# Branch B's recurrence in a hybrid decoder block: per-chunk transition matrices in place of a chunk-by-chunk solve

## The chip, the cores and the metric

The kernel runs on one core of a Trainium2 chip. A core has TensorE (PE; its weight loads are listed as PEld), VectorE (DVE), ScalarE (ACT), GpSimd (POOL) and SyncE (SP), which here issues nearly all DMAs. Every engine works through its own instructions in a fixed order and waits on semaphores. The metric is device microseconds of one execution; lower is better.

## The reference

The block is one decoder layer over 16 learned tokens and 1024 tokens of width 1024: a half-step SwiGLU, then two mixers side by side (A, a gated DeltaNet with 8 heads of 128; B, RWKV-7 with 16 heads of 64), their gated sum through an output projection, a second half-step SwiGLU and a norm. The change concerns B's recurrence:

```python
def step(state, inp):
    r_t, w_t, k_t, v_t, a_t, b_t = inp
    sa = jnp.einsum('bhvk,bhk->bhv', state, a_t)
    state = state * w_t[:, :, None, :] + sa[..., None] * b_t[:, :, None, :] \
        + v_t[..., None] * k_t[:, :, None, :]
    return state, jnp.einsum('bhvk,bhk->bhv', state, r_t)
```

Per head the state is 64 x 64. Each token multiplies it by a decay, adds a rank-one term that depends on the state itself (`sa`) and one that does not, and reads an output out of it. Everything is float32.

## The kernel before, in words

The program has three stages: `ffn1`, `middle`, `ffn2`. Activations lie transposed, channels on partitions and tokens along the free axis. `middle` handles two segments of tokens (528 with the learned ones, then 512), and in each, one after another, eight channel blocks j of 128: one head of A and two heads of B, B's first head on partitions 0 to 63, its second on 64 to 127. Each pair of segment and j is a round `it`, sixteen in all.

A round's actions are written as functions, and `schedule()` (L162) gives their program order: `merge_blocks chains new_b+ new_a+ operands+ inverses+ gates finish`, where + marks the next round's. The order at the segment change (`SWITCH`) and in the last round (`FINAL`: `gates merge_blocks chains fill finish`, where `fill` is the output projection of the first segment) differ. That order is not the order of execution. A planner sorts each engine's instructions when the program is built: of what it takes to be ready by its own estimate, the one that is earliest in program order goes first. So `chains` of one round goes ahead of everything of the next, and where it waits by that estimate, projections (`pp`, 128x128 weights, 24 matmuls for one column tile and 512 tokens) and `operands` of the next round are put between its pieces. The order so found is fixed at run time.

**new_b, new_a** (L925, L1019) project and prepare B's and A's inputs. **operands** (L1060) makes, for all chunks of a round, the products that need no state: for B in chunks of CB = 64 tokens (NCB = 8 chunks), `LT` (from `grb`, L1076), `BKt` (transposes of `BK`, L1145), and in a loop over three kinds (L1154) `vka`, `yb` and `vbk`, the last multiplied by the chunk's decay `gam`. **inverses** (L1209) and **merge_blocks** (L1252) make the triangular inverses `Y` of all chunks, 64 x 64 for B, 128 x 128 for A, by way of DRAM (`scX`, `Xc`).

**chains** (L1292) runs through the chunks in order. `chunk_a` (four of them, 128 tokens each) and `chunk_b` (eight) are independent chains that alternate: B's chunk i, then A's chunk i/2 if i is even. `chunk_b` (L1347) takes the state `SB` (128 partitions x 64: two heads), and does, each for two heads by two 64x64 matmuls: `b1` = AR·SB; on DVE `rh` = b1 + vka; `b2` = Y·rh; on ACT `U`, its copy out of PSUM; `b3` = BKt·U; on DVE the new state, b3·gam + sg, where POOL has made sg = SB·gam + vbk meanwhile; and the outputs `bq` = SB·AR + U·LT, added to `yb` on DVE. Each product has a PSUM tile of the pool `ch`, which has two banks and also serves `merge_blocks`, `chunk_a` and `finish`. The pool `mx`, which `operands` uses, has two banks in the first segment and three in the second. A head's matmul with both operands on partitions 0 to 63 and its output there uses one quadrant of the PE array, the other head's the opposite one; the index pairs `HS` and `HX` choose the quadrants.

**gates, finish** (L1386, L1413) make the gates and the norms of both outputs and store the merged round; `finish` uses `yb`, and of the chain's tiles `BKt` as scratch.

Each fp32 matmul leaves two records in the trace.

## Time and profile before

| | us |
|---|---|
| median of 3 runs | 3180.59 |
| lowest, highest | 3179.36, 3185.57 |
| the profiled execution | 3186.03 |
| its span, first to last instruction | 3184.2 |
| one round of the second segment (1889.42 to 1979.64) | 90.22 |
| mean granted TensorE clock | 0.984 |

The profile page is one execution. Its second part shows the span in 40 slices, as tenths of busy time:

```profile
PE   5999999999999999999999999999999899999998
DVE  7554444346676676676767777777766755555335
ACT  4222222125555555454565455555544422222114
```

`middle` lies between slices 12 and 31: the first product of `chunk_b` starts at 914.9 us, the last one at 2399.5 us. A group of instructions (by line, engine, operation and tile) has its count after x, its busy time, the mean of one in ns, and the idle time of the engine before them. The chain that ended last is listed as pieces with a start, a length and a line. A row of windows gives a stretch, its length, and for PE, PEld, DVE, ACT and POOL the busy time with the number of instructions, then the granted clock, the share of DMA and GB/s.

### The profile page before, as it was taken

How to read it: one execution, taken by the hardware profiler on the slowest of the kernel's cores; microseconds unless marked ns; L12 is line 12 of the kernel's file. 1: busy time of each engine (PE TensorE's matmuls, PEld its weight loads, DVE VectorE, ACT ScalarE, POOL GpSimd, SP SyncE). 2: the span in 40 equal slices, each digit the busy share in tenths (PEclk: the TensorE clock that was granted, in tenths of full speed). 3: DMA queues.
4: the chain of work that ended last, by engine and by line, in shares of the span. 5: the costliest groups of instructions: out<-in, count | busy, mean ns of one | idle time of the engine just before them, and what ended most of it. 6: DMA issues, size and time to landing. Idle time of an engine off the chain costs nothing. (4 is left out here: it accounts for less than half of the span.)

```text
span 3184.2 us, 57962 instructions
## 1 busy us (share of the span) xinstructions
PE 3048.8 (96%) x23606; PEld 2523.7 (79%) x23606; DVE 1950.6 (61%) x3820; ACT 1321.8 (42%) x2260; POOL 551.2 (17%) x810
## 2 busy tenths in 40 slices
PE   5999999999999999999999999999999899999998
PEld 4999998998877877787776777777776688887886
DVE  7554444346676676676767777777766755555335
ACT  4222222125555555454565455555544422222114
POOL 4222220000011011110111111111101433222000
PEclk8999999999999999999999999999999999999999
DMA  2222224234222222222332232233344232224323
GB/s 93 95 93 81 81 84 160 77 94 143 60 68 72 74 72 59 72 71 75 96 92 71 70 82 71 71 79 78 96 149 165 67 99 86 80 82 150 104 79 111
DMA packets 256554, 286.93 MB, mean 90 GB/s; under 512 B 168272, under 2 KB 174416, under 8 KB 256288
## 3 DMA queue, kind: packets, MB, share of 16 engines
q1 hardware_dynamic: 252048, 271.42, 28.9%
q0 software_dynamic: 2512, 8.65, 0.7%
q8 instruction: 185, 3.03, 0.4%
q10 hardware_dynamic: 1728, 3.16, 0.3%
q14 instruction: 81, 0.66, 0.1%
HBM read 232.70 MB, written 50.47 MB: 89 GB/s over the span
## 5 line engine op out<-in xcount | busy, mean ns | idle before, releaser
L259 PE MATMUL pp<-uk,w 128*128 128x264 f32 (+1 forms) x4824 | 994.8, 354 | 7.6 <-DVE gg L1410 3.9
L259 PEld LDWEIGHTS pp<-uk,w 128*128 128x128 f32 x4824 | 747.8, 191 | 130.7 <-issue 22.1
L154 ACT ACTIVATE w<-wraw 128x1024 fp32r<-128x1024 f32 (+2 forms) x332 | 328.2, 989 | 709.8 <-PE pd L259 289.9
L259 PE MATMUL pd<-hd,w 128*128 128x512 f32 (+1 forms) x2640 | 499.6, 351 | 12.6 <-DVE w L155 5.7
L259 PEld LDWEIGHTS pd<-hd,w 128*128 128x128 f32 x2640 | 428.6, 189 | 82.4 <-DVE w L155 7.2
L422 PE MATMUL pg<-bt,w 128*128 128x260 f32 (+1 forms) x2772 | 456.8, 321 | 24.3 <-ACT bt L154 10.1
L422 PEld LDWEIGHTS pg<-bt,w 128*128 128x128 f32 x2772 | 400.3, 189 | 69.4 <-ACT bt L154 11.0
L428 DVE TENSOR_TENSOR c<-c,pg 128x520 f32<-128x520 f32 (+1 forms) x308 | 208.0, 689 | 361.3 <-PE pg L422 296.5
L155 DVE TENSOR_TENSOR w<-wraw,w 128x1024 fp32r<-128x1024 f32 (+2 forms) x332 | 382.6, 1153 | 67.6 <-ACT w L154 61.4
L422 PE MATMUL pg<-b,w 128*128 128x260 f32 (+1 forms) x2376 | 390.1, 320 | 10.1 <-POOL b L155 4.9
L422 PEld LDWEIGHTS pg<-b,w 128*128 128x128 f32 x2376 | 343.8, 189 | 45.1 <-POOL b L155 5.4
L392 POOL TENSOR_TENSOR wrx<-wrx 128x512 f32<-128x512 f32 x44 | 66.7, 1515 | 574.8 <-DVE w22b L155 306.5
L154 ACT ACTIVATE w<-wrx 128x1024 fp32r<-128x1024 f32 (+1 forms) x66 | 60.3, 913 | 182.6 <-PE pg L422 169.4
L1357 POOL TENSOR_SCALAR sgam<-SBn,gam 128x64 f32<-128x64 f32 x112 | 66.7, 595 | 393.1 <-DVE SBn L1371 371.7
L1230 DVE TENSOR_TENSOR Xb<-Xb,tb 115x126 f32<-115x126 f32 (+22 forms) x496 | 126.2, 254 | 11.9
L1228 DVE TENSOR_TENSOR tb<-Ub,Xb 115x126 f32<-115x126 f32 (+22 forms) x496 | 125.2, 252 | 11.0
L1039 DVE SCALAR_TENSOR_TENSOR acc<-xr,pk,acc 128x528 f32<-128x528 f32 (+1 forms) x144 | 108.8, 755 | 18.9 <-ACT acc L1035 17.5
L539 DVE SCALAR_TENSOR_TENSOR h<-pd,h 128x528 f32<-128x528 f32 (+1 forms) x64 | 44.6, 698 | 117.7 <-PE pd L259 117.7
L259 PE MATMUL pwo<-uk,w 128*128 128x512 f32 x384 | 106.2, 421 | 6.2 <-ACT rg L918 2.7
L539 DVE SCALAR_TENSOR_TENSOR hh<-pd,hh 128x512 f32<-128x512 f32 x64 | 44.2, 690 | 107.8 <-PE pd L259 106.7
L259 PEld LDWEIGHTS pwo<-uk,w 128*128 128x128 f32 x384 | 72.5, 196 | 26.0 <-ACT rg L918 3.5
L1371 DVE SCALAR_TENSOR_TENSOR SBn<-b,gam,sgam 128x64 f32<-128x64 f32 x128 | 36.2, 283 | 88.7 <-PE b L1354 87.6
(373 smaller groups left out, 4045.5 us busy)
## 6 DMA issues: line engine op xcount, KB each, us to landing
wraw<-in_win SPq DMA_DIRECT2D x150, 512.0 KB, 3.7
wraw<-in_wgu SPq DMA_DIRECT2D x44, 512.0 KB, 3.5
wrx<-in_wgu SPq DMA_DIRECT2D x44, 512.0 KB, 3.7
wraw<-in_wdn SPq DMA_DIRECT2D x48, 320.0 KB, 3.0
wraw<-in_wdn SPq DMA_DIRECT2D x32, 384.0 KB, 3.1
hid<-c SPq DMA_DIRECT2D x44, 260.0 KB, 4.0
hr<-hid SPq DMA_DIRECT2D x22, 520.0 KB, 9.9
hid<-c SPq DMA_DIRECT2D x44, 256.0 KB, 3.2
```

The lines of the kernel that those rows point to most:

```text
L154: g.nc.scalar.activation(hi, src, AF.Copy)
L155: (eng or g.nc.vector).tensor_tensor(lo, src, hi.bitcast(F32), op=ALU.subtract)
L259: g.nc.tensor.matmul(ps, lhsT=l, rhs=r, start=i == 0, stop=i == n - 1)
L392: nc.gpsimd.tensor_tensor(a22, a21, a22, op=ALU.add)
L422: nc.tensor.matmul(ps[:, c0 : c0 + cn], lhsT=l[:, x, k, :], rhs=r[:, k, y, c0 : c0 + cn], start=i == 0, stop=i == 3 * HK - 1)
L428: nc.vector.tensor_tensor(o, x, y, op=ALU.add)
L539: nc.vector.scalar_tensor_tensor(hv, pd, 0.5, hv, op0=ALU.mult, op1=ALU.add)
L1039: nc.vector.scalar_tensor_tensor(acc[:, :n], xr[:, tap : tap + n], V("convw", ct * 4 + tap), acc[:, :n], op0=ALU.mult, op1=ALU.add)
L1228: nc.vector.tensor_tensor(tv, U[:, i, i + 1 :].unsqueeze(2).to_broadcast([npt, nt, ncc]), X[:, i, 0:ncc].unsqueeze(1).to_broadcast([npt, n ...
L1230: nc.vector.tensor_tensor(X[:, i + 1 :, 0:ncc], X[:, i + 1 :, 0:ncc], tv, op=ALU.add)
L1357: nc.gpsimd.tensor_scalar(sg, SB, gam, None, op0=ALU.mult)
L1371: nc.vector.scalar_tensor_tensor(new, p3[:, :CB], gam, sg, op0=ALU.mult, op1=ALU.add)
```

## The change

For a chunk, the new state is an affine function of the old one. The change computes its matrix and its constant part for all eight chunks ahead, in a new function `transitions` that `chains` calls first, so that in series there is one product a chunk, and the outputs follow for all chunks at the end.

In `operands`, `at`, the transpose of AR's first half, is made by products with the identity, its matmuls alternating with those of `vka`; `yb` and `vbk` form the second alternating pair, and `vbk` leaves PSUM without the factor `gam`. In `transitions` there are six products over all chunks and both heads (32 records each): xa = Y·at and xv = Y·vka, copied out by ACT; mt = xa·BKt plus the unit matrix; vbk += BKt·xv, then times `gam` on POOL; AR's second half += xa·LT; yb += xv·LT (the four additions on DVE). A step is then: one product mt·SB of two 64x64 matmuls, and on DVE the new state product·gam + vbk. The states of all chunks are kept in `SBs`. After the loop, `bq` = SBs·AR over all chunks and one addition to `yb`. The tile `unit` is filled once, at the start of `middle`.

```diff
--- before.py
+++ after.py
@@ -722,6 +722,10 @@
         g.Ub = ms.tile([115, 32, 32], F32, name="Ub")
         for t in (*g.Y, g.XA, g.Ub):
             nc.gpsimd.memset(t, 0.0)
+
+        g.unit = ms.tile([P, CB], F32, name="unit")
+        for hp in HS:
+            nc.gpsimd.tensor_copy(g.unit[hp], g.C("ident")[hp, hp])
         g.bkpm = ms.tile([P, 2, 64], F32, name="bkpm")
         nc.gpsimd.memset(g.bkpm, 0.0)
         g.bkm = ms.tile([P, 64], F32, name="bkm")
@@ -1138,6 +1142,7 @@
     inverse_inputs(g, q)
 
     BKt = q.BKt = st.tile([P, NCB, 2, CB], F32, name="BKt", tag="BKt", bufs=2)
+    at = q.at = st.tile([P, NCB, CB], F32, name="at", tag="at")
     ps = [g.mx.tile([P, 512], F32, name="bkt", tag="mx") for _ in range(2)]
     for i in range(NCB):
         for y in range(2):
@@ -1148,19 +1153,29 @@
         nc.scalar.activation(BKt[:, :, y], ch3(ps[y], CB), AF.Copy)
 
     Vs = q.Vs
-    vka = q.vka = st.tile([P, NCB, CB], F32, name="vka", tag="vka")
-    vbk = q.vbk = st.tile([P, NCB, CB], F32, name="vbk", tag="vbk")
+    vka, vbk = (st.tile([P, NCB, CB], F32, name=x, tag=x) for x in ("vka", "vbk"))
+    q.vka, q.vbk = vka, vbk
     yb = q.yb = st.tile([P, FULL], F32, name="yb", tag="yb", bufs=2)
-    for kind in range(3):
-        ps = g.mx.tile([P, 512], F32, name="vp", tag="mx")
+
+    def kind(name, *ops):
+
+        ps = [g.mx.tile([P, 512], F32, name=name, tag="mx") for _ in ops]
         for i in range(NCB):
-            for hp, hx in HX:
-                l, r = ((LT[hx, i, 1, :CB], Vs[hx, i]), (Vs[hx, i], LT[hx, i, 1, CB:]), (BKt[hx, i, 1], Vs[hx, i]))[kind]
-                nc.tensor.matmul(ps[hp, i * CB : (i + 1) * CB], lhsT=l, rhs=r, start=True, stop=True)
-        if kind == 2:
-            nc.vector.tensor_tensor(vbk, ch3(ps, CB), q.gam.unsqueeze(2).to_broadcast([P, NCB, CB]), op=ALU.mult)
-        else:
-            nc.scalar.activation(yb if kind else vka.rearrange("p c m -> p (c m)"), ps, AF.Copy)
+            for p, op in zip(ps, ops):
+                for hp, hx in HX:
+                    l, r = op(i, hp, hx)
+                    nc.tensor.matmul(p[hp, i * CB : (i + 1) * CB], lhsT=l, rhs=r, start=True, stop=True)
+        return ps
+
+    ident = g.C("ident")
+    pa, pv = kind("vp", lambda i, hp, hx: (AR[hp, i, 0, :], ident[hp, hp]),
+                  lambda i, hp, hx: (LT[hx, i, 1, :CB], Vs[hx, i]))
+    nc.scalar.activation(at, ch3(pa, CB), AF.Copy)
+    nc.scalar.activation(vka, ch3(pv, CB), AF.Copy)
+    pr, pk = kind("vp", lambda i, hp, hx: (Vs[hx, i], LT[hx, i, 1, CB:]),
+                  lambda i, hp, hx: (BKt[hx, i, 1], Vs[hx, i]))
+    nc.scalar.activation(yb, pr, AF.Copy)
+    nc.scalar.activation(vbk, ch3(pk, CB), AF.Copy)
     if meta:
         btm = q.btm = st.tile([64, P], F32, name="btm", tag="btm")
         ps = g.mx.tile([P, 512], F32, name="btp", tag="mx")
@@ -1289,15 +1304,45 @@
     nc.vector.tensor_copy(Y[0:64, NCB:, 64:128], ch3(ps4[0:64, 0:256], 64))
 
 
+def transitions(g, q):
+
+    nc, st = g.nc, g.st
+    Y = g.Y[q.it % 2]
+    AR, LT, BKt, vbk, yb = q.AR, q.LT, q.BKt, q.vbk, q.yb
+    flat = lambda t: t.rearrange("p c m -> p (c m)")
+
+    def product(pool, name, op):
+        ps = getattr(g, pool).tile([P, 512], F32, name=name, tag=pool)
+        for i in range(NCB):
+            for hp in HS:
+                l, r = op(i, hp)
+                nc.tensor.matmul(ps[hp, i * CB : (i + 1) * CB], lhsT=l, rhs=r, start=True, stop=True)
+        return ps
+
+    xa, xv = (st.tile([P, NCB, CB], F32, name=x, tag=x) for x in ("xa", "xv"))
+    nc.scalar.activation(flat(xa), product("ch", "xp", lambda i, hp: (Y[hp, i, hp], q.at[hp, i])), AF.Copy)
+    nc.scalar.activation(flat(xv), product("ch", "xp", lambda i, hp: (Y[hp, i, hp], q.vka[hp, i])), AF.Copy)
+    mt = q.mt = st.tile([P, NCB, CB], F32, name="mt", tag="mt")
+    ps = product("ch", "mp", lambda i, hp: (xa[hp, i], BKt[hp, i, 0]))
+    nc.vector.tensor_tensor(mt, ch3(ps, CB), g.unit.unsqueeze(1).to_broadcast([P, NCB, CB]), op=ALU.add)
+    ps = product("ch", "np", lambda i, hp: (BKt[hp, i, 0], xv[hp, i]))
+    nc.vector.tensor_tensor(vbk, ch3(ps, CB), vbk, op=ALU.add)
+    nc.gpsimd.tensor_tensor(vbk, vbk, q.gam.unsqueeze(2).to_broadcast([P, NCB, CB]), op=ALU.mult)
+    ps = product("ch", "rp", lambda i, hp: (xa[hp, i], LT[hp, i, 0, CB:]))
+    nc.vector.tensor_tensor(AR[:, :, 1, :], ch3(ps, CB), AR[:, :, 1, :], op=ALU.add)
+    ps = product("ch", "yp", lambda i, hp: (xv[hp, i], LT[hp, i, 0, CB:]))
+    nc.vector.tensor_tensor(yb, ps, yb, op=ALU.add)
+
+
 def chains(g, q):
 
+    transitions(g, q)
     nc, st, c, j = g.nc, g.st, q.c, q.j
     meta = q.s == 0
     Y = g.Y[q.it % 2]
     S, SB = q.SA, q.SB
     Va, ktl, attn, egl = q.Va, q.ktl, q.attn, q.egl
     kqg = q.kq[:, :, q.off : q.off + FULL]
-    AR, LT, BKt = q.AR, q.LT, q.BKt
     hs = lambda h: slice(64 * h, 64 * h + 64)
     pt = lambda name: g.ch.tile([P, 512], F32, name=name, tag="ch")
     if meta:
@@ -1324,7 +1369,6 @@
         nc.tensor.matmul(ps[:, :P], lhsT=q.vkm[:, 1, :], rhs=vnm, start=True, stop=True)
         nc.vector.tensor_copy(S, ps[:, :P])
     oa = q.oa = kqg[:, 1, :]
-    yb, vka, vbk = q.yb, q.vka, q.vbk
 
     def chunk_a(i):
         csl = slice(i * CA, (i + 1) * CA)
@@ -1344,43 +1388,26 @@
         nc.vector.scalar_tensor_tensor(S, S, egl[:, i : i + 1], p3[:, :P], op0=ALU.mult, op1=ALU.add)
         nc.scalar.activation(oa[:, csl], pq[:, :CA], AF.Copy)
 
-    def chunk_b(i, SB):
-        gam, csl = q.gam[:, i : i + 1], slice(i * CB, (i + 1) * CB)
-
-        def mm(ps, *terms):
-
-            for k, (l, r) in enumerate(terms):
-                for hp in HS:
-                    nc.tensor.matmul(ps[hp, :CB], lhsT=l[hp], rhs=r[hp], start=k == 0, stop=k == len(terms) - 1)
-
-        sg = st.tile([P, CB], F32, name="sgam", tag="sgam", bufs=1)
-        nc.gpsimd.tensor_scalar(sg, SB, gam, None, op0=ALU.mult)
-        nc.gpsimd.tensor_tensor(sg, sg, vbk[:, i], op=ALU.add)
-        p1 = pt("b1")
-        mm(p1, (AR[:, i, 0, :], SB))
-        rh = st.tile([P, CB], F32, name="rhB", tag="rhB", bufs=1)
-        nc.vector.tensor_tensor(rh, p1[:, :CB], vka[:, i], op=ALU.add)
-        p2 = pt("b2")
+
+    SBs = st.tile([P, NCB + 1, CB], F32, name="SBs", tag="SBs")
+    nc.gpsimd.tensor_copy(SBs[:, 0], SB)
+    for i in range(NCB):
+        ps = pt("b1")
         for hp in HS:
-            nc.tensor.matmul(p2[hp, :CB], lhsT=Y[hp, i, hp], rhs=rh[hp], start=True, stop=True)
-        U = st.tile([P, CB], F32, name="Us", tag="Us", bufs=2)
-        nc.scalar.activation(U, p2[:, :CB], AF.Copy)
-        p3 = pt("b3")
-        mm(p3, (BKt[:, i, 0], U))
-        new = st.tile([P, CB], F32, name="SBn", tag="SBn", bufs=2)
-        nc.vector.scalar_tensor_tensor(new, p3[:, :CB], gam, sg, op0=ALU.mult, op1=ALU.add)
-        pq = pt("bq")
-        mm(pq, (SB, AR[:, i, 1, :]), (U, LT[:, i, 0, CB:]))
-        nc.vector.tensor_tensor(yb[:, csl], pq[:, :CB], yb[:, csl], op=ALU.add)
-        return new
-
-    for i in range(NCB):
-        SB = chunk_b(i, SB)
+            nc.tensor.matmul(ps[hp, :CB], lhsT=q.mt[hp, i], rhs=SBs[hp, i], start=True, stop=True)
+        nc.vector.scalar_tensor_tensor(SBs[:, i + 1], ps[:, :CB], q.gam[:, i : i + 1], q.vbk[:, i],
+                                       op0=ALU.mult, op1=ALU.add)
         if i % 2 == 0:
             chunk_a(i // 2)
+    ps = pt("bq")
+    for i in range(NCB):
+        for hp in HS:
+            nc.tensor.matmul(ps[hp, i * CB : (i + 1) * CB], lhsT=SBs[hp, i], rhs=q.AR[hp, i, 1, :],
+                             start=True, stop=True)
+    nc.vector.tensor_tensor(q.yb, ps, q.yb, op=ALU.add)
     if meta:
         nc.sync.dma_start(g.sdr[j][:, :P], S)
-        nc.sync.dma_start(g.sdr[j][:, P:], SB)
+        nc.sync.dma_start(g.sdr[j][:, P:], SBs[:, NCB])
 
 
 def gates(g, q):
```

## The prediction

> **What bounds the kernel now.** The page's first part and the windows come first: is one engine full in the stage that changes, or does the chain of state updates set the pace?
>
> ```profile
> PE 3048.8 (96%) x23606; PEld 2523.7 (79%) x23606; DVE 1950.6 (61%) x3820; ACT 1321.8 (42%) x2260; POOL 551.2 (17%) x810
> ```
> ```profile
> 1889.42:1979.64 90.22, 89.46 (x831) 66.33 (x832) 66.38 (x164) 49.19 (x92) 14.61 (x31) 1.00 0.31 79
> ```
> The second row is one whole round of the middle stage (one head index j of the second segment): 90.22 us, PE busy 89.46 of it, at granted clock 1.00; DVE 66.38, ACT 49.19. The round is PE's. While the chain of head j waits, PE runs the projections (`pp`) and operands of head j+1. So a shorter chain buys nothing by itself: what counts is PE time. The next view, the chain that ended last, shows what PE time a chunk costs (start, length, what).
>
> ```profile
> 1918.96 0.22 PE p L1332 x2
> 1919.18 0.94 PE pp L259 x4
> 1920.12 0.22 PE p L1336 x2
> 1920.34 0.22 PE pq L1340 x2
> 1920.56 0.47 PE pp L259 x2
> 1921.03 0.26 PE pq L1341 x2
> 1921.29 0.22 PE p L1343 x2
> 1921.51 0.70 PE pp L259 x3
> 1922.21 0.26 PE b L1354 x4
> 1922.47 0.66 PE pp L259 x2
> 1923.13 0.26 PE b L1365 x4
> 1923.39 0.67 PE pp L259 x2
> 1924.06 0.26 PE b L1354 x4
> 1924.32 0.23 PE bq L1354 x8
> 1924.55 0.43 PE pp L259
> ```
> ```profile
> 1950.19 1.92 PE vp L1159 x65
> ...
> 1952.69 12.16 PE pp L259 x52
> ```
> The reader is to see four prices. (1) A projection matmul in a run: 12.16 / 52 = 0.234 us. After one of A's groups it costs that as well (0.94 for 4). (2) After a group of B's it does not: 2 take 0.66 where 0.47 is due, 1 takes 0.43. So **each return from 64x64 matmuls to 128x128 ones costs 0.19 us**. (3) In a run, a record of B's 64x64 kind (one matmul leaves two records) costs 1.92 / 65 = 0.0295; a group of 4 right after projections takes 0.26 instead of 0.12: 0.14 to enter. One excursion of B costs 0.33 besides its work. (4) A chunk of A is 0.22 + 0.22 + 0.22 + 0.26 + 0.22 = 1.14 and pays no such price.
>
> A chunk of B makes three excursions (`b` L1354; `b` L1365; `b` and `bq` together): 3 x 0.26 + 0.23 + 3 x 0.19 = 1.58 us for 0.59 of work (20 records). The last round confirms it, where nothing but wout's `pwo` stands between the chunks:
>
> ```profile
> 2363.90:2399.90 36.00, 36.00 (x280) 24.21 (x278) 14.31 (x39) 9.02 (x21) 6.10 (x14) 1.00 0.47 160
> ```
> ```profile
> L259 PE MATMUL pwo<-uk,w 128*128 128x512 f32 x82 | 28.4, 437 | 0.0
> ```
> 36.0 - 82 x 0.234 (19.2) - 4 x 1.14 (4.6) = 12.2 us for eight chunks; 8 x 1.58 = 12.6, of which the first `b` (0.45) stands mostly ahead of the window. So among projections B costs 12.6 a round.
>
> **The change, part by part.** It removes, per round, `chunk_b`'s 80 matmuls (160 records, 4.7 us of work) in 24 excursions. It adds six products of 32 records, 8 steps of 4, one output run of 32, and 32 records for `at`: 288, or 128 more. PE has more work and fewer excursions.
>
> *Transitions.* If the six products stand in one run: 6 x 32 x 0.0295 = 5.66, and one excursion of 0.33: 6.0 us. *Steps:* 8 x (0.26 + 0.19) = 3.6; projections still stand between them, since each waits for the scalar_tensor_tensor of the one before. *Outputs:* 0.94 + 0.33 = 1.27. *`at`* is issued alternately with `vka`, and its rows and columns of the array are the two quadrants that `vka` leaves free. The nearest row with four quadrants in turn is `bkt`'s (start, length):
>
> ```profile
> 1556.91 0.98 PE L1145 MATMUL bkt<-ck,BK 64*64 64x64 f32 x52
> 1557.83 0.97 PE L259 MATMUL pp<-uk,w 128*128 128x512 f32 x3
> ```
> 0.92 / 52 = 0.0177 each, so the pair takes 64 x 0.0177 = 1.13 instead of 0.94: +0.19 (at most +0.94, if the quadrants don't overlap; I take 0.19, the same pattern). Sum added: **11.1 us**.
>
> *What is removed in an ordinary round.* Three chunks stand among projections (up to 1932.5), 3 x 1.58 = 4.7. The other five stand among the next head's `grb`, `bkt` and `vp`, 64x64 as well: such a chunk costs between its work (0.59) and 1.58, so 3.0 to 7.9. I take the middle, 5.4, as excursions are partly shared there but stalls come in. Removed: **10.2** (7.7 to 12.6). Against 11.1 that is +0.9.
>
> *A's chunks move.* With the chain done earlier, A's last two leave that stretch too, six groups whose excursions (0.33 each, up to 2.0) go; I take -1.0, half.
>
> *Evacuations and waits.* The prices:
>
> ```profile
> L1163 ACT ACTIVATE vka<-vp 128x512 f32<-128x512 f32 x16 | 9.6, 597 | 7.3 <-PE vp L1159 6.8 <-DVE rhB L1362 0.4
> L1161 DVE TENSOR_TENSOR vbk<-vp,gam 128x512 f32<-128x512 f32 x16 | 11.1, 691 | 38.9 <-PE vp L1159 36.7 <-POOL sgam L1358 1.5 <-POOL ELx L962 0.8
> L1109 POOL TENSOR_TENSOR E<-E,tk 128x512 f32<-128x512 f32 x16 | 16.8, 1051 | 13.8 <-ACT E L1103 9.9 <-ACT kts L1106 3.9
> L1367 ACT ACTIVATE Us<-b 128x64 f32<-128x64 f32 x128 | 28.6, 224 | 128.3 <-PE b L1365 128.0
> L1362 DVE TENSOR_TENSOR rhB<-b,vka 128x64 f32<-128x64 f32 x128 | 28.3, 221 | 21.2 <-PE b L1354 16.2
> L1374 DVE TENSOR_TENSOR yb<-bq,yb 128x64 f32<-128x64 f32 x128 | 27.5, 214 | 0.0
> L1358 POOL TENSOR_TENSOR sgam<-sgam,vbk 128x64 f32<-128x64 f32 x128 | 52.7, 412 | 22.4 <-DVE vbk L1161 12.5
> L1357 POOL TENSOR_SCALAR sgam<-SBn,gam 128x64 f32<-128x64 f32 x112 | 66.7, 595 | 393.1 <-DVE SBn L1371 371.7 <-DVE yb L1374 17.2 <-DVE tb L1228 4.2
> ```
> DVE: -8 x (0.221 + 0.214) - 0.69, +5 x 0.69 = -0.7 us a round. ACT: -8 x 0.224, +4 x 0.60 = +0.6. POOL: -8 x (0.60 + 0.41), +1.05 and a copy = about -7. None of the three is the bound, and no DMA is added or moved (the state's store keeps its place and size; `unit` is two copies, once). Only what they do to PE counts. Five of the six products wait for a bank or an operand that ACT (0.60) or DVE (0.69) must first evacuate, while PE runs the product before it (0.94): covered with 0.25 to spare, if the engine is free. It may be in one of the splits of weights:
>
> ```profile
> L154 ACT ACTIVATE w<-wraw 128x1024 fp32r<-128x1024 f32 (+2 forms) x332 | 328.2, 989 | 709.8 <-PE pd L259 289.9
> L155 DVE TENSOR_TENSOR w<-wraw,w 128x1024 fp32r<-128x1024 f32 (+2 forms) x332 | 382.6, 1153 | 67.6 <-ACT w L154 61.4
> ```
> Then 0.69 + 1.15 - 0.94 = 0.9 late: 0 to 4.5 us for five; I take 1.0, as DVE is in a split in about a tenth of a round (9 x 1.15 of 90) and otherwise in shorter work. The cover is the product itself; where it goes, a projection put in costs 0.33. In turn an `mt` or `vbk` add waiting at the head of DVE holds the split queued behind it, for which the projections wait; and `vbk`'s multiply on POOL holds the next head's `xr` copies by up to 1 us, which their convolution's slack takes up. Step 0's state needs that multiply (0.69 + 1.05 after its product); the two products behind (1.9) cover it. In the first segment `mx` has two banks, and each pair of `kind` needs both: up to two evacuations of 0.60 stand bare, twice; a projection put in makes that 0.33 each, inside the 1.0.
>
> **Sum:** +0.9 - 1.0 + 1.0 = +0.9 for 15 rounds, 13.5; in the last round 11.1 - 12.6 + 0.5 of stalls = -1.0. Together **+12 us**. The profiled execution took 3186.03 (its span is 3184.2): 3198. The median of the runs shown is 3180.59: **3192**.
>
> One wait could move as well:
>
> ```profile
> PE iv L1263 <- DMA Xc<-scX: 18.7, 7, 3.2
> ```
> In the first segment PE reaches `merge_blocks` before the inverses have come back from DRAM, 2.7 us in each of seven rounds. With no chain between the operands and that point PE may come earlier still, or the order may put more projections ahead: -18.7 to +18.7. I take 0; no row says which, and both ends are in the range.
>
> **The rivals.** *A, faster:* every excursion saved counts fully, the products run without a stall. Each of the 16 rounds gets the last one's 11.1 - 12.6 = -1.5: -24, so 3157. For it: that round's window; and PE's busy share covers some 8 us of entering and returning (24 x 0.33) in a round. Against it: five of eight chunks stand where excursions are shared. The Trainium skill's page Perfetto Trace Analysis, Identifying the Most-Contended Engine, holds that matmul busy share is no measure of how full PE is and that the weight-load share is; the trace has 79% there beside 96%. That speaks for A. *B, balance:* the sum above, 3175 to 3210. *C, slower:* the products don't run together. Each waits for its evacuation, and the order fills the gap with projections, so that every cut costs an excursion: five more, 1.65, and `at`'s and `kind`'s pairs cost 0.6 more. That decides once an evacuation ends later than the 0.94 of the product before it. +0.9 + 1.65 + 0.6 = 3.1 a round, 16 times 50: 3230. The skill's page TensorEngine Tiling (Array Packing), PSUM Bottleneck, says that tiling makes the matmuls quicker and not the emptying of PSUM, which may then be the limit. By it C is the outcome; the rows have 0.69 against 0.94, so not unless DVE is late. *D:* the chain becomes shorter as the change says and nothing else moves, which is B without its terms, 3181: inside B.
>
> **How the numbers follow.** A 0.30, B with D 0.47, C 0.23. What a measurement can tell from no change is 0.2%, 6.4 us: 3174 to 3187. A is faster; B straddles, a third of it (0.16) within, 0.02 below and the rest above; C is slower; of A 0.03 and of C 0.01 falls within. Faster 0.29, same 0.20, slower 0.51. The range takes in A with some of the gain in `Xc`, and C: 3150 to 3235. B alone is 3175 to 3210.
>
> **What would show it.** Right: some 290 B records a round in place of 160; six products in a run near 6 us; eight groups of 4 followed by a projection piece 0.19 too long; rounds of about 91 us. Rival A: rounds under 89. Rival C: projections between the `xp`, `mp`, `np`, `rp`, `yp` groups, or PE idle released by the adds on DVE; rounds of 93. The prediction is wrong if PE's time doesn't follow from records and excursions at all: if the wait for `Xc` or for split weights changes by more than the rounds do.

## The result, and the profile after

| | before | after |
|---|---|---|
| median, us | 3180.74 (4 runs) | 3201.99 (4 runs) |
| lowest, highest | 3179.36, 3185.57 | 3200.44, 3202.52 |
| the profiled execution, its span | 3186.03, 3184.2 | 3201.6, 3199.8 |

The kernel became slower by 0.63%: ratio 1.0063, 95% interval 1.0046 to 1.0081. Between the two profiled executions it is 15.6 us, between the medians 21.2; the profiled execution of before lies 5.3 above its median, and that part stands in no trace.

The first part of the page of after (busy time, share of the span, instructions):

```profile
PE 3064.5 (96%) x25654; PEld 2578.9 (81%) x25654; DVE 1950.8 (61%) x3628; ACT 1330.9 (42%) x2196; POOL 457.8 (14%) x588
```

PE has 2048 records more, which is 16 rounds of 128, and 15.7 us more busy time, as much as the span grew. DVE and ACT hardly changed, POOL lost 93 us, and none of that shows in the time: PE was the bound and still is.

Where does it stand? A window over five rounds of the second segment, from one `gat<-g` to the fifth after it, first before, then after. The columns are the stretch, its length, busy time with count for PE, PEld, DVE, ACT and POOL, the granted clock, DMA share and GB/s.

```profile
1875.17:2326.33 451.16, 447.35 (x4141) 331.68 (x4140) 332.38 (x813) 245.23 (x460) 72.86 (x153) 1.00 0.31 83
```
```profile
1890.36:2346.10 455.74, 448.50 (x4782) 344.67 (x4780) 331.72 (x753) 250.91 (x441) 43.90 (x82) 1.00 0.30 82
```

A round takes 455.74 / 5 = 91.15 us against 90.23: +0.92. Only 0.23 of it is PE's busy time (448.50 - 447.35, by 5). PE's idle time went from 3.81 to 7.24 in five rounds, +0.69 a round. The 641 records more are paid for almost wholly by excursions and records that went; what isn't paid for is waits.

One wait stands out. In three of the five rounds PE stands 0.44, 1.57 and 0.46 before `gra` (the products of the next head of A), 2.47 together and more than half of the 4.6; before has no such wait. The round with 1.57, on the timelines of after (SPq is SyncE's queue of DMA issues):

```profile
2048.44 0.33 SPq L1200 DMA_DIRECT2D SB<-sdr  x1
2048.82 1.48 SPq L1416 DMA_DIRECT2D ugr<-in_upg  x1
2052.08 0.31 ACT L154 ACTIVATE ug<-ugr 128x128 fp32r<-128x128 f32 x1 [2.37 <-DMA ugr<-in_upg]
2054.00 1.13 PE L1121 MATMUL gra<-kq 128*128 128x256 f32 x4 [1.57 <-DVE LT L1083]
```

The loop now starts with a copy of the state into `SBs`, on POOL. It waits until PE has read the outputs of the round before out of `SBs` (1.00 us of POOL's time, up to 2048.18), and the load of a later state (`SB`) waits for that copy (1.6 us on SyncE's queue). Behind this load in SyncE's queue stands the load for `ug`, a weight of `gates`. In before it goes out 6.4 us ahead of the round's first `LT` (2019.80 and 2026.23), here 0.7 (2048.82 and 2049.54). ACT and DVE wait for `ug`, and on DVE the second half of `LT` stands behind it, for which `gra` waits. The last two rounds have no state left to load and no such wait, and take 90.55 and 90.37. No run took the wait out by itself.

The same anchor (`gat<-g`) through the whole program splits the 15.6 us:

| stretch | before | after | difference |
|---|---|---|---|
| start to the first round's `gat` | 951.76 | 960.38 | +8.6 |
| six rounds of the first segment | 619.01 | 623.98 | +5.0 |
| three rounds around the change of segment | 304.40 | 306.00 | +1.6 |
| five rounds of the second segment | 451.16 | 455.74 | +4.6 |
| the rest | 857.9 | 853.7 | -4.2 |

The fourteen rounds of the three middle rows cost 11.2, 0.80 each. The first round alone costs 8.6, and the end gives 4.2 back.

The six products in an ordinary round, on the timeline of after (start, length, engine, what, idle time before it and who ended it); the first, `xp<-at,Y`, begins at 1929.0 among the last `iv` and isn't shown:

```profile
1930.17 1.15 PE L1319 MATMUL xp<-vka,Y 64*64 64x64 f32 x32
1931.20 1.15 PE L1319 MATMUL mp<-BKt,xa 64*64 64x64 f32 x32
1932.63 1.15 PE L1319 MATMUL np<-xv,BKt 64*64 64x64 f32 x32 [0.28 <-ACT xv L1324]
1933.71 1.12 PE L921 MATMUL cs<-sg,ones 128*128 128x512 f32 x2
1934.77 1.15 PE L1319 MATMUL rp<-LT,xa 64*64 64x64 f32 x32
1935.75 1.10 PE L1319 MATMUL yp<-LT,xv 64*64 64x64 f32 x32
1936.71 0.33 PE L1397 MATMUL b<-SBs,mt 64*64 64x64 f32 x4
```

Ends are modelled, so starts are to be compared: 0.96 to 1.08 from one group to the next, but 1.43 from `mp` to `np`, with a stall of 0.28 in it; one foreign group. Then the steps, with projections between them:

```profile
1940.76 0.33 PE L1397 MATMUL b<-SBs,mt 64*64 64x64 f32 x4
1941.02 0.97 PE L259 MATMUL pp<-uk,w 128*128 128x512 f32 x3
1941.92 0.33 PE L1397 MATMUL b<-SBs,mt 64*64 64x64 f32 x4
```

A step is 0.26 to the next start, and three projections behind it take 0.90 where 0.70 is due: 0.20 for the return.

The first round is another matter. Behind its products, on the same view of after:

```profile
916.30 1.15 PE L1319 MATMUL yp<-LT,xv 64*64 64x64 f32 x32
918.29 0.39 PE L1352 MATMUL bm<-uvm,ltm 16*16 16x64 f32 x4 [0.84 <-DVE AR L1332]
918.61 0.87 PE L1080 MATMUL grb<-AR,BK 64*64 64x128 f32 x18
919.82 0.39 PE L1357 MATMUL bm<-rhm,ym 16*16 16x64 f32 x4 [0.34 <-DVE rhm L1354]
```

The block for the learned tokens (`bm`, `am`) now stands behind the transitions and waits on DVE, 0.84 and 0.34. Then the granted clock goes to half, by the windows of after, and of before for the same stretch:

```profile
920.00:934.00 14.00, 14.00 (x88) 8.73 (x85) 4.47 (x13) 1.27 (x4) 0.35 (x4) 0.53 0.03 5
```
```profile
920.00:934.00 14.00, 13.42 (x202) 9.37 (x201) 7.51 (x26) 5.71 (x15) 2.11 (x6) 1.00 0.31 79
```

In 14 us at a clock of 0.53 PE gets through 88 records, before through 202 at 1.00. At (1 - 0.53) x 14 = 6.6 us, this is most of the first round's 8.6.

### The profile page after: what moved, and what is told of

It reads as the page before. It is cut to its first block, busy times and chain, and to the rows that moved or that the text cites. A ratio compares the mean times of both kernels' runs of the same rounds, so it can differ in the third digit from the quotient of the medians.

```text
span 3199.8 us, 61487 instructions
## 1 busy us (share of the span) xinstructions
PE 3064.5 (96%) x25654; PEld 2578.9 (81%) x25654; DVE 1950.8 (61%) x3628; ACT 1330.9 (42%) x2196; POOL 457.8 (14%) x588
## 4 chain that ended last, share of the span: by engine, by line
PE 62%; DVE 5%; ACT 3%; DMA 2%; issue 2%; POOL 1%; SPq 0%; DVEq 0%; POOLq 0%; ACTq 0%
PE pp L259 24%; PE pg L422 12%; PE pd L259 7%; PE pwo L259 3%; PE cs L921 2%; PE vp L1167 1%; DMA Xc<-scX 1%; PE b L1397 1%; PE gra L1121 1%; PE grb L1080 1%; PE p L1376 1%; PE bkt L1150 1%; PE pq L1385 1%; DVE w L155 1%; PE iv L1278 1%
## 5 line engine op out<-in xcount | busy, mean ns | idle before, releaser
L259 PEld LDWEIGHTS pp<-uk,w 128*128 128x128 f32 x4824 | 751.7, 192 | 122.5 <-issue 21.2
L1243 DVE TENSOR_TENSOR tb<-Ub,Xb 115x126 f32<-115x126 f32 (+22 forms) x496 | 125.1, 252 | 11.9 <-DMA Ub<-scr 0.2
L259 PE MATMUL pwo<-uk,w 128*128 128x512 f32 x384 | 99.1, 409 | 6.2 <-ACT rg L922 2.7
L839 ACT ACTIVATE sh<-pp,pk 128x528 f32<-128x528 f32 (+1 forms) x54 | 37.2, 690 | 126.9 <-PE pp L259 115.8
L154 ACT ACTIVATE hd<-hr 128x1040 fp32r<-128x1040 f32 (+1 forms) x44 | 45.4, 1061 | 79.1 <-DMA hr<-hid 52.6
```

Of the source, the lines that this page charges most:

```text
L154: g.nc.scalar.activation(hi, src, AF.Copy)
L259: g.nc.tensor.matmul(ps, lhsT=l, rhs=r, start=i == 0, stop=i == n - 1)
L839: nc.scalar.activation(sh[:, 1 : 1 + n], ps, AF.Identity, scale=g.V("mu", i))
L1243: nc.vector.tensor_tensor(tv, U[:, i, i + 1 :].unsqueeze(2).to_broadcast([npt, nt, ncc]), X[:, i, 0:ncc].unsqueeze(1).to_broadcast([npt, n ...
```

## The experiments

Twelve kernels. "Rounds" is the mean of five rounds of the second segment, taken as above; there the clock is 1.00, or 0.99, in every run, so this number shows the price of an edit more sharply than the total does. It has a scatter too: the five rounds of before, e5 and e6 agree to 0.1 us, but those of most others lie 1.6 to 2.3 us apart. Ratios are to the kernel before on the same chip; its median there lay between 3180.7 and 3187.1, so totals are better compared by ratios than by medians.

| run | median, us | ratio (95%) | rounds, us |
|---|---|---|---|
| before | 3180.74 | 1 | 90.23 |
| after | 3201.99 | 1.0063 (1.0046 to 1.0081) | 91.15 |
| e1_meta_first | 3186.48 | 1.0010 (1.0002 to 1.0019) | 91.36 |
| e2_out_with_step | 3207.79 | 1.0082 (1.0067 to 1.0097) | 92.11 |
| e3_no_products | 3091.55 | 0.9715 (0.9701 to 0.9730) | 84.76 |
| e4_full_step | 3192.83 | 1.0031 (1.0018 to 1.0045) | 90.76 |
| e5_before_full_b2 | 3176.61 | 0.9976 (0.9965 to 0.9986) | 89.91 |
| e6_operands_part | 3199.53 | 1.0042 (1.0030 to 1.0054) | 91.47 |
| e7_first_and_full | 3183.94 | 1.0006 (0.9995 to 1.0017) | 90.85 |
| e8_wide_step | 3203.24 | 1.0061 (1.0048 to 1.0074) | 92.16 |
| e9_first_full_wide | 3187.29 | 1.0009 (1.0001 to 1.0018) | 90.70 |
| e10_scy_act | 3246.85 | 1.0202 (1.0183 to 1.0222) | 92.68 |
| e11_b2_scy_act | 3193.38 | 1.0034 (1.0020 to 1.0047) | 91.16 |
| e12_kinds_apart | 3191.45 | 1.0018 (1.0009 to 1.0027) | 90.95 |

### The parts of the change

**e3**: after, without the six products.

```diff
-    nc.scalar.activation(flat(xa), product("ch", "xp", ...), AF.Copy)
...
-    nc.vector.tensor_tensor(yb, ps, yb, op=ALU.add)
+    q.mt = q.at
```

> The changed kernel without the six products of transitions and their evacuations (the steps take at as their matrix, vbk keeps its multiply by gam on POOL; the output is not the reference's). Theory 1 (PE time adds up): 6.0 us a round and 1.0 of stalls go, 16 x 7 = 112 us: 3090 (3085 to 3106 with stalls between 0 and 1.3). Theory 2 (the products lie in time that PE would partly spend waiting): 50 us or less, 3150 or more.

110 us less than after, 6.9 a round; in the rounds of the second segment 91.15 - 84.76 = 6.4. The waits of `gra` account for the gap: e3 has 5.16 us of them in its five rounds, after 2.47, and without them it is 90.65 - 83.73 = 6.9 there too. The products cost what records say, 6 x 32 x 0.0295 and an entry, with some waits. The price is additive: PE has no slack that would take them in.

**e6**: before, with only the operand part (`at` beside `vka`, the other two kinds in a pair; `vbk` keeps its factor `gam` on DVE).

```diff
-    for kind in range(3):
-        ps = g.mx.tile([P, 512], F32, name="vp", tag="mx")
...
+    pa, pv = kind("vp", lambda i, hp, hx: (AR[hp, i, 0, :], ident[hp, hp]),
+                  lambda i, hp, hx: (LT[hx, i, 1, :CB], Vs[hx, i]))
...
+    pr, pk = kind("vp", ...)
```

> The kernel before with only the operand part of the change: the sixteen products that give A's transpose (at), and the products of the kinds interleaved two by two; the chain of chunks stays as it was and doesn't use at. By records: 32 records in a run and two entries less, +0.19 to +0.6 a round, so 3184 to 3191 on a base of 3181. If the first rounds' loss (+12 at the second round) comes from this part, which delays the branch's operands in ACT's and DVE's queues: 3190 or more with the half-clock stretch near 920 us in its trace. If it is free: 3181.

3199.5, past the first range: the smallest part of the change by itself brings two thirds of the whole loss (0.42% of 0.63%). The second condition did not hold: no half-clock stretch near 920 us is in its trace (its first `gat` is at 955.73). It is in every round, by the window over five of them:

```profile
1884.64:2341.99 457.35, 451.48 (x4301) 335.20 (x4300) 332.75 (x815) 248.36 (x466) 70.99 (x153) 1.00 0.30 82
```

+1.24 a round: 0.83 of PE's busy time and 0.41 of idle. The timeline of e6 shows the idle part, in the middle of the operand products:

```profile
1960.06 0.63 PE L1163 MATMUL vp<-LT,Vs 64*64 64x64 f32 x15
1961.19 0.68 PE L1163 MATMUL vp<-Vs,BKt 64*64 64x64 f32 x16 [0.51 <-ACT at L1169]
```

The second pair needs two free PSUM banks before its records can alternate, and the second bank comes free only when ACT has copied `at` out. From the first `vp` to `ktp`, the group behind, e6 takes 4.85 us in four of five rounds, before 3.81. Of these 1.04 more, 0.67 are the second pair's: its 64 records take 2.68 us (1960.05 to 1962.73), in before 2.01 (1950.03 to 1952.04). It gains no overlap either, as `yb` and `vbk` both use the quadrants of `HX`: where they alternate, 28 records take 0.82 us (1961.70 to 1962.52), 0.029 each as in a run. The first pair costs the other 0.37, for 32 more records.

**e12**: e1 (below), with the four products each by itself.

```diff
-    pa, pv = kind("vp", lambda ..., lambda ...)
+    pa, = kind("vp", lambda i, hp, hx: (AR[hp, i, 0, :], ident[hp, hp]))
+    nc.scalar.activation(at, ch3(pa, CB), AF.Copy)
+    pv, = kind("vp", lambda i, hp, hx: (LT[hx, i, 1, :CB], Vs[hx, i]))
...
```

> The kernel after with the transition products behind the learned-token block (3186.5 by itself, rounds of the second segment 91.36 us), and with the four products of the operand part each by itself in the order at, vka, yb, vbk, instead of interleaved two by two. Theory 'stalls' (the operand part costs 1.24 a round where 0.19 was forecast, since a pair waits for BKt and for two banks before its first record, 0.3 and 0.5 a round, while its records overlap as forecast): 128 records at 0.0295 = 3.8 us without waits against about 3.9 with them, rounds 91.0 to 91.4, and 3180 to 3187. Theory 'records' (the waits would come anyway and the overlap of the pair's quadrants is lost): +0.75 a round, so about 92.1 and 3198.

Theory "stalls", by the rounds: 90.95 against 91.36, and the operand part takes 3.89 in four of five rounds instead of 4.25 or more. The overlap of `at` and `vka` is real (28 records in 0.40 us where they alternate in e1, 0.0145 each), but the second pair, which has nothing to overlap, and the pairs' waits cost more than it brings. The total did not follow: the ratios are 1.0018 and 1.0010, and their intervals overlap. In the traces e12's six rounds of the first segment take 620.4 against 612.3, and 4.8 of that is a wait of PE (what for, us in total, times, longest), first e1, then e12:

```profile
PE iv L1278 <- DMA Xc<-scX: 12.9, 7, 3.0
```
```profile
PE iv L1278 <- DMA Xc<-scX: 17.7, 7, 3.3
```

What a round of the first segment saves ahead of `merge_blocks` can come back as a longer wait for `Xc`.

**e2**: after, with the outputs of a chunk beside its step instead of in one run.

```diff
+        ps = pt("bq")
+        for hp in HS:
+            nc.tensor.matmul(ps[hp, :CB], lhsT=SBs[hp, i], rhs=q.AR[hp, i, 1, :], start=True, stop=True)
...
```

> The changed kernel with one part undone: a chunk's output product is issued with its step again (8 groups of 4 records and 8 small additions on DVE a round in place of one run of 32 and one addition of 0.69). Theory 1 (an excursion from the projections to 64x64 matmuls costs 0.33 us): beside the step it needs no excursion of its own, and the run's goes: 16 x 0.33 = 5 us less, 3197. Theory 2 (only records count): 3202. If the order puts each output apart from its step, theory 1 has 7 excursions more a round, 37 us, 3239, and theory 2 still 3202.

3207.8, between "records" and "apart". Its timeline shows why:

```profile
1944.70 0.33 PE L1397 MATMUL b<-SBs,mt 64*64 64x64 f32 x4
1944.96 0.49 PE L259 MATMUL pp<-uk,w 128*128 128x512 f32 x1
1945.38 0.33 PE L1402 MATMUL bq<-AR,SBs 64*64 64x64 f32 x4
1945.64 0.50 PE L259 MATMUL pp<-uk,w 128*128 128x512 f32 x1
```

Six of the eight stand apart, each with its 0.26 and about 0.19 for the return: 2.7 us. Gone are the run of outputs, 1.08, and the waits of `gra` for `LT`, 0.49 a round in after. That is +1.1; the rounds show +0.96.

### The first round and the clock

**e1**: after, with `transitions` called behind the learned-token block.

```diff
-    transitions(g, q)
     nc, st, c, j = g.nc, g.st, q.c, q.j
...
         nc.vector.tensor_copy(S, ps[:, :P])
+    transitions(g, q)
```

> The changed kernel with the call of transitions moved behind the learned tokens' small products (bm, am) of the first segment; nothing else differs. Theory 1 (part of the loss is the clock): in the changed kernel's first round the six products stand ahead of those small ones, PE waits 0.84 and 0.34 us for them with nothing else to run, and the granted clock is 0.50 from 920.3 to 934 us, which costs 6.8 us. With the small products first the episode goes: 3202 - 8 = 3194. Theory 2 (the loss is only records against excursions): the same work, so 3202 (3199 to 3205).

3186.5, twice the gain expected. Its clock from 920 to 940 us:

```profile
920.00:940.00 20.00, 19.70 (x273) 15.11 (x270) 10.21 (x32) 3.40 (x11) 1.12 (x3) 1.00 0.11 22
```

The half-clock stretch is gone, and the first `gat` comes at 953.73 instead of 960.38. But the next six rounds, from that anchor on, take 612.3 us against 624.0, and only the first segment has a learned-token block. There `bm`'s waits are gone (2.7 in the rows of after), less clock is lost ((1 - clock) x time from 780 to 2440 us is 17.1 against 32.4), and `Xc` is waited for 1.5 us less. The clock is no accident of the traced executions: over the whole span it is 0.980 or 0.981 in all four of after, 0.983 to 0.986 in the eleven of e1. The second segment is no better, 91.36. So the place of one call in `chains` is worth some 15 us, all of it in the first segment. The change still costs its 1.1 a round in the second, and e1 comes out close to before by what it saves in waits and clock.

Is the order alone to blame for the clock? **e8** (edit below) keeps after's order, and to within 0.2 us its timeline from 911 to 921 us is the same, with the same two waits:

```profile
918.48 0.39 PE L1352 MATMUL bm<-uvm,ltm 16*16 16x64 f32 x4 [0.84 <-DVE AR L1332]
920.00 0.39 PE L1357 MATMUL bm<-rhm,ym 16*16 16x64 f32 x4 [0.34 <-DVE rhm L1354]
```
```profile
922.00:926.00 4.00, 4.00 (x37) 2.62 (x36) 1.95 (x5) 0.37 (x1) 0.13 (x4) 1.00 0.01 2
```

The same window of after:

```profile
922.00:926.00 4.00, 4.00 (x16) 2.24 (x13) 1.86 (x4) 0.00 (x0) 0.00 (x0) 0.50 0.00 0
```

16 records instead of 37, at half the clock. So the order makes the fall possible and something else decides; the traces of e2 and e4 have it, that of e8 hasn't. The Trainium skill, TensorE: Matmul & The Clock Gate, What's actually happening, says that the clock is set by a free-running window of activity of about 3.4 us, so that the same work falls in it differently. The traces agree: in each of the fourteen, all half-clock stretches begin whole steps of 3.413 us apart, to 4 ns, and the steps lie differently in each. In after a step runs from 917.41 to 920.82, takes in both waits, and the fall is at its end; in e8 a step ends at 918.68, between them. One step and the time behind it in after, then the two steps of e8:

```profile
917.41:920.82 3.41, 2.23 (x40) 1.46 (x38) 2.25 (x6) 0.27 (x1) 0.00 (x0) 1.00 0.02 5
920.83:924.23 3.40, 3.40 (x20) 1.87 (x17) 1.74 (x5) 0.36 (x1) 0.35 (x4) 0.50 0.00 0
```
```profile
915.27:918.68 3.41, 2.57 (x84) 2.43 (x78) 2.86 (x6) 0.09 (x1) 1.04 (x1) 1.00 0.00 0
918.68:922.09 3.41, 3.07 (x47) 1.74 (x44) 2.06 (x6) 0.63 (x2) 0.31 (x4) 1.00 0.02 5
```

How much idle time in a step brings a fall isn't shown: steps with up to 1.9 us of it pass, and the fall of e2 follows one with 0.66.

**e10** and **e11** meant to shorten the `Xc` waits: the two stores of `scY`, which stand ahead of `Xc`'s load in SyncE's queue, go out from ScalarE's; e10 on after, e11 on e5.

```diff
-        nc.sync.dma_start(scY[:nblk, :, r, :], Yt[64 * r : 64 * r + nblk])
+        nc.scalar.dma_start(scY[:nblk, :, r, :], Yt[64 * r : 64 * r + nblk])
```

> The kernel after with the two stores of scY issued from ScalarE's queue instead of SyncE's, where they stand between the store of scX and the load of Xc. Theory 'wait and clock': the seven waits of iv for Xc in the first segment (14.4 us) shorten by 1 to 2 us each, and the half-clock stretches behind them (1.7 to 3.4 us lost each) become fewer: -10 to -25, so 3177 to 3192, and the rounds of the second segment, which have no such wait, stay at 91.15. Theory 'records': the waits are cover that something else takes, 3200 or more; ScalarE's own stall while it issues (about 4 us for the two on SyncE's queue) may even add.

> The kernel before with both edits that are not the change: b2 as one 128x128 matmul (3176.6 alone), and the stores of scY from ScalarE's queue. Theory 'wait and clock': 18.7 us of Xc waits shrink by 1 to 2 us each and clock is regained: 3155 to 3170. Theory 'records': 3177.

Both theories fell: +45 and +17 us on their bases. ScalarE stands still while it issues, on the timeline of e10 (ACTq is its queue of DMA issues):

```profile
985.22 4.83 ACTq L1250 DMA_DIRECT2D scY<-Yt  x2
990.16 0.70 ACT L839 ACTIVATE sh<-pp,pk 128x528 f32<-128x528 f32 x1 [8.08 <-PE pp L259]
```

`sh` and, at 990.76, a split of weights stand behind the 4.83 us (the rest of the 8.08 is ACT's wait before the issue), and what PE makes of them behind those. In e10 the `Xc` waits (us in total, times, longest) grew to

```profile
PE iv L1278 <- DMA Xc<-scX: 27.1, 7, 5.0
```

from 14.4, and the clock lost between 780 and 2440 us, (1 - clock) x time over windows of 2 us, from 32.5 to 49.5. So wait and clock do grow together, +12.7 and +17, but the edit made them worse. How much a shorter wait would bring wasn't shown.

### The price of an excursion

The prediction took 0.33 for going from 128x128 to 64x64 and back, and so for a matter of tile size. **e4**: after, the step as one 128x128 matmul on a block-diagonal matrix (zeros outside its two blocks), so that the size never changes in a step.

```diff
-        for hp in HS:
-            nc.tensor.matmul(ps[hp, :CB], lhsT=q.mt[hp, i], rhs=SBs[hp, i], start=True, stop=True)
+        nc.tensor.matmul(ps[:, :CB], lhsT=g.mt[:, i, :], rhs=SBs[:, i], start=True, stop=True)
```

> The changed kernel with the transition matrices of the two heads in one block-diagonal 128x128 tile (zeros elsewhere, set once), so that a step is one 128x128 matmul in place of two 64x64 ones; the addition that fills it becomes two of 0.69 us on DVE. Theory 1 (the way to 64x64 matmuls and back is what a step costs): a step takes about 0.11 in place of 0.46 us, 16 x 8 x 0.35 = 45 us less, 3157, below the kernel before. Theory 2 (only the streamed columns count): 0.11 in place of 0.12 a step, 2 us less, 3200.

3192.8, -0.39 a round: a miss. Its rounds hold more of `gra`'s waits, 4.14 us in five against 2.47; without them it is -0.73, where eight steps at 0.14 less (below) would make -1.1. The step on its timeline:

```profile
1931.75 0.43 PE L1399 MATMUL b<-SBs,mtz 128*128 128x64 f32 x2
1931.99 0.94 PE L259 MATMUL pp<-uk,w 128*128 128x512 f32 x3
1932.77 0.33 PE L1399 MATMUL b<-SBs,mtz 128*128 128x64 f32 x2
```

0.24, and 0.78 for three projections where 0.70 is due: 0.32 instead of 0.46, though half the records and no change of size are left. The Trainium skill, TensorEngine Tiling (Array Packing), Key Properties, has it that a change of tiling mode drains the engine. That is not the larger part here: without any change 0.32 of 0.46 stays.

**e8**: after, the two 64x64 matmuls of a step on 128 columns, the state before beside the one used. **e9**: e7 (e1 and e4 together) with the same widening.

```diff
+        lo = max(i - 1, 0)
+        w = (i + 1 - lo) * CB
...
-            nc.tensor.matmul(ps[hp, :CB], lhsT=q.mt[hp, i], rhs=SBs[hp, i], start=True, stop=True)
+            nc.tensor.matmul(ps[hp, :w], lhsT=q.mt[hp, i], rhs=SBs[hp, lo : i + 1]..., start=True, stop=True)
```

> The kernel after with the step's two 64x64 matmuls on 128 columns instead of 64 from the second chunk on (the state before stands beside the one used; its columns are computed and dropped). Theory 'records': each record costs by its columns, 0.0295 -> 0.059, on top of a fixed toll of 0.33: 7 x 16 x 0.118 = +13, so 3215. Theory 'load': the longer stream covers as much more of the next weight load as it takes, so a step keeps its 0.46 with what follows it: 3202 within 3.

> The kernel after with two edits together: the transition products behind the learned-token block, and the chunk's step as one 128x128 matmul on a block-diagonal matrix. If the two gains add (3186.5 - 9.2): 3177, below the kernel before. If the second gain was only a luckier clock: 3186.

> The run with both edits (transitions behind the learned-token block, step as one 128x128 matmul), and that one matmul on 128 columns instead of 64 from the second chunk on. Theory 'load': the step becomes like one of branch A's groups, which take 0.22 and leave the projections behind them at 0.234: 0.32 -> 0.22, 7 x 16 x 0.10 = -11 from the run with both edits, so about 3166. Theory 'columns': 64 more columns of fp32 stream 0.107 more: +12 from it, about 3189.

By its total, e8 speaks for "load" (+1 us). By its rounds it speaks for "records": 92.16, +1.0, sixteen times of which would be 16 us. A step takes 0.36 to the next start instead of 0.26:

```profile
1938.80 0.44 PE L1399 MATMUL b<-SBs,mt 64*64 64x128 f32 x4
1939.16 0.96 PE L259 MATMUL pp<-uk,w 128*128 128x512 f32 x3
```

What hid it in the trace is the first segment: the first `gat` comes 4.9 us earlier than in after, with the clock at 1.00, and the six rounds behind it take 3.4 less. e7 gains 0.51 a round on e1, but the rounds of each lie 1.6 to 1.9 apart, and 2.5 us in all, which is not clear of noise. (Its traced execution, 3197, stands 13 above the median and loses 11.9 us to a half clock from 1763 to 1787 us, behind a wait of 2.2; so the median can't be explained by that.) In e9 doubling the columns costs nothing, 90.70 against 90.85, and also gains nothing like the 11 us expected. So a 64x64 group pays a toll and its columns besides; a 128x128 one costs about 0.3 between projections, with 64 columns and with 128 (in e9 0.24, and 0.79 for three projections). What makes this floor, the weight load or something else, was not measured apart.

**e5**: before, `b2` by the whole block-diagonal inverse.

```diff
-        for hp in HS:
-            nc.tensor.matmul(p2[hp, :CB], lhsT=Y[hp, i, hp], rhs=rh[hp], start=True, stop=True)
+        nc.tensor.matmul(p2[:, :CB], lhsT=Y[:, i, :], rhs=rh, start=True, stop=True)
```

> The kernel before with b2's two 64x64 matmuls replaced by one 128x128 matmul on the whole block-diagonal inverse (zeros outside its two blocks, so the result is unchanged). 16 x 8 groups. Theory 'mode' (the price of an excursion is the change of tile size, as the prediction had it): a group falls from 0.45 to the 0.11 that 64 columns stream, -0.34 x 128 = -44, so 3137. Theory 'load' (the price is a short fp32 matmul whose neighbours' weight loads are not covered, whatever its size; the wide step of the second trace took 0.32 instead of 0.46): -0.14 x 128 = -18, so 3163. Theory 'chain' (something other than PE sets the rounds): 3181.

3176.6, ratio 0.9976: the one version that beats both kernels, by less than any theory but the last. Its timeline, among projections and then among the next head's 64x64 work:

```profile
1922.74 0.33 PE L1364 MATMUL b<-rhB,Y 128*128 128x64 f32 x2
1922.88 0.71 PE L259 MATMUL pp<-uk,w 128*128 128x512 f32 x2
1923.52 0.33 PE L1354 MATMUL b<-Us,BKt 64*64 64x64 f32 x4
...
1932.39 0.43 PE L1076 MATMUL grb<-AR,BK 64*64 64x128 f32 x2
1932.75 0.43 PE L1364 MATMUL b<-rhB,Y 128*128 128x64 f32 x2
1933.11 0.45 PE L1076 MATMUL grb<-AR,BK 64*64 64x128 f32 x8
```

Among projections: 0.14, and 0.64 for two where 0.47 is due, so 0.31 against 0.45. Between groups of `grb` it takes 0.36, where four 64x64 records would take 0.12 at the run's price. A round has chunks of both kinds, and -0.32 is left of the -1.1 that theory "load" gives.

## Why the prediction was right, and where not

It held: slower, 3192 forecast and 3202 measured, by rival B's mechanism. The rise itself, 21.2, is nearly twice the 12 forecast. The balance of its terms came out, +0.9 forecast and +0.92 measured for a round, but not each term:

| term, us a round | forecast | measured |
|---|---|---|
| the six products with their stalls | 6.0 + 1.0 | 6.9 (e3, total, and rounds without `gra`'s waits) |
| `at` and the pairs | 0.19 | 1.24 (e6) |
| steps, outputs | 3.6 + 1.27 | 0.46 a step and 1.08 a run in the trace of after |
| `gra`'s waits behind the late load for `ug` | 0 | 0.49 |
| removed, with A's chunks | 10.2 + 1.0 | 12.6, what is left |
| sum | +0.9 | +0.92 |

**`at` and the pairs** are the step that was most mis-sized. The prediction took 0.19, from the rate of `bkt`, and named up to 0.94 if the quadrants do not overlap. They do overlap, at 0.37 for the pair. The second pair, of `yb` and `vbk`, was put at nothing and takes 0.67: it shares its quadrants, so nothing overlaps, and it waits 0.51 for a bank, which the prediction had only for the first segment ("each pair of `kind` needs both" banks, there inside the 1.0). Where the last 0.20 of 1.24 stand wasn't found.

**The late load.** The prediction says "no DMA is added or moved". None is added, but the state's load moved behind the copy into `SBs`, and the load for `ug` with it; on average that is 0.49 a round. **What is removed** was taken in the middle between 3.0 and 7.9 for the five chunks among 64x64 work, with half of A's 2.0. With steps and outputs at their forecast, the sum leaves 0.92 = 1.24 + 6.9 + 4.87 + 0.49 - 12.6, above the middle that was taken (11.2; the ends are 7.7 and 14.6). No run took it by itself, so it holds what is wrong in the other terms. Costs of 1.05 and 0.49 too little and a saving of 1.4 too little cancel; that the sum came within 0.02 is luck.

**The excursion.** The toll of 0.33 was right as a price: entries of 0.14 and returns of 0.19 to 0.20 stand in the traces of after and e2. As an explanation (returns "from 64x64 matmuls to 128x128 ones") it fell for the larger part with e4 and e5: without a change of size 0.32 of 0.46 and 0.31 of 0.45 stay.

**The first round** was not in the prediction. It costs 8.6 instead of 0.9, by the learned-token block's waits and a half clock behind them. The prediction took the granted clock as 1.00 from a round of the second segment and let it stand for all rounds; "if the wait for `Xc` ... changes by more than the rounds do" was on its list of what would make it wrong, and the clock was not. **The wait for `Xc`**, left at 0 with both signs open, fell from 18.7 to 14.4; the clock lost between 780 and 2440 us rose from 25.6 to 32.5 meanwhile, mostly in the first round.

**The last round** was forecast at -1.0 and the end came out at -4.2. B's part is what was forecast, by the window of after that takes in products, steps and outputs:

```profile
2385.90:2411.40 25.50, 25.50 (x347) 20.31 (x345) 12.71 (x26) 6.86 (x14) 1.04 (x1) 1.00 0.40 139
```

Less 44 `pwo` at 0.234 (10.3) and four chunks of A at 1.14 (4.6), 10.6 us are B's, against 10.9 forecast without `at`, and 12.2 in before. Another 3.4 is clock: before loses 1.7 at 2418 us where after loses nothing, and 3.4 at 2448 where after, at 2467, loses 1.7. That is 0.8 more than the 4.2; where after loses the 0.8 is open.

**Rival A** (3157) needed each excursion to count fully, also among 64x64 work; rounds of 91.15 exclude it. **Rival D** (3181) had nothing else moving; the ratio of 1.0046 or more excludes it. **Rival C** (3230) needed the products cut up by projections. They stand in one run with one stall of 0.28. The order that it feared is there in another place: the pairs wait for their evacuations, at 1.24 instead of C's 0.6 more.

## What to carry to other kernels

Where one engine is full, count what each part adds to that engine and measure the parts one by one: here the balance was right to 0.02 us a round while two of its terms were wrong by about 1, and the smallest edit (two interleaved pairs) cost more a round, 1.24, than the whole change. Interleaving two products for the sake of the array's quadrants needs both PSUM banks at once and brings nothing where both use the same quadrants. Follow a new copy's waits into the DMA queues: here one on POOL, which is idle most of the time, cost PE 0.49 a round by way of a load that has nothing to do with it. A total that moves by less than some 15 us doesn't price an edit in a kernel with stretches at half clock: the place of one call was worth that much in e1, the twelve executions of e4 alone lie between 3184.8 and 3203.5 (clock 0.983 and 0.975), and e8's total hid 1.0 us a round that only windows at a clock of 1.00 showed.

## What the runs showed of the hardware

- The clock falls to half after short waits, not only long ones. In after, each of the six longer waits for `Xc` in the first segment, of 1.5 to 2.8 us, is followed by 1.7 or 3.4 us lost to a half clock; and 1.2 us of waits in two pieces were followed by 6.8 us lost. The Trainium skill, TensorE: Matmul & The Clock Gate, Why this matters for your kernels, asks for no gaps of more than about 3 us; these rows have falls after half of that.
- After the same records and waits at the same times, to 0.2 us, the clock went to 0.50 in one kernel (after) and stayed at 1.00 in another (e8). In every trace the half-clock stretches begin on a grid of 3.413 us, which lies elsewhere in each execution.
- 64x64 records in four quadrants in turn cost 0.0145 to 0.0177 us each, in two 0.029 to 0.0295, also where two products that share them alternate; between long 128x128 ones, a group of four 64x64 records on 64 columns costs 0.46 with the return, one of two 128x128 records on 64 columns 0.31 to 0.32.
- Issuing two DMAs of 102 KB each held ScalarE's queue for 4.83 us (e10), and what stood behind it on that engine came that much later.
